# A token mixer's weight blocks on ScalarE's DMA queue, its products in another order, and later stages' loads further ahead

## The chip, the cores and the metric

The kernel runs on one core of one Trainium2 chip. A core has TensorE (matrix products), VectorE, ScalarE and GpSimd, and SyncE, which here only issues DMAs; ScalarE and GpSimd can issue DMAs too. Each engine works through its own instructions in a fixed order, and a wait of one instruction holds all behind it. The metric is the time of one execution on the device in microseconds.

## The reference

One encoder block on 1024 tokens of 1024 channels in float32: half a gated feed-forward layer, a mixer, another half of a feed-forward layer, a gated embedding, a norm. Cut to the mixer, which is what changes:

```python
u = rms_norm(h, mix_norm[i])
z = u @ w_in[i]                       # q | k | v | s_in | gates: 512 each, gates 2 x 1024
y_attn = neighbourhood_attention(q, k, v, na_rpb[i]) @ w_attn_out[i]   # 8 heads, 16 x 64 grid
y_ssm = s5_branch(s_in, ...) @ w_ssm_out[i]                            # scans in both directions
g_attn, g_ssm = jnp.split(jax.nn.sigmoid(gates), 2, axis=-1)
h = h + (g_attn * y_attn + g_ssm * y_ssm) @ w_out[i]

def s5_branch(s_in, ...):             # 32 groups of 16 channels, each a 64-dim complex state
    y = d_skip * u + forward scan + backward scan
    y = jax.nn.gelu(y)
    return y * jax.nn.sigmoid(y @ glu_w + glu_b)       # the gated unit
```

## The kernel before

Activations stand with channels on the 128 partitions and 512 tokens (one of two halves, t) on the free axis. Every float32 operand is split into a high and a low part (`split`: a cast on ScalarE, a subtraction on VectorE), and a product is three matmuls (`mm3`, lines 190 to 192): high x high, high x low, low x high.

The large products are done by a seven-product scheme on 2 x 2 blocks. In the mixer a "pair" is two column groups of `w_in` (q with k, or two gate groups), 12 pairs in all, and an item is one of the seven products of a pair: 84 items of 4 steps, a step being one `mm3`. Product i takes an activation operand `A7[i]`, a weight operand made by `b_operand` from four weight blocks (b11, b12, b21, b22; tile `blk`, 256 KB each), and adds into one of three PSUM banks:

```python
A7 = ("a12", "a11", "s1", "s2", "s4", "s3", "a22")
ACC7 = "ZXYXYXX"
NEW7 = (True, True, True, False, False, False, False)
```

Product 0 needs b21, product 1 b11, product 2 b12 - b11, 3 then b22 - b11, 4 b22, 5 b22 - b12, 6 b21 less what b11 became (`b_operand` changes the blocks in place, line 428 and 430). `s_evac` copies a finished bank or adds it to what was copied and hands results to `s_out`; q and k go to DRAM (`q_d`, `k_d`) from ScalarE's queue, the gates (`g_d`) from SyncE's. The stores wait in a list, `later`, which `s_store` issues in the third step of the next item. `s_ahead(n)` issues the block loads of items up to n + 4 (`s_load`, line 1490, SyncE's queue) and prepares weights up to n + 2 (`s_prep`). Blocks, prepared weights, results and much of attention's data share one pool of 24 buffers of 128 x 512 (tag "m"); a load waits until the buffer that it is given is free.

Between the steps of the items, side work runs from a generator, `mixer_side`: each step calls `tick`, and `yield n` lets n steps pass before the generator goes on. Its stages, in order:

- *injection*: for each of 16 pairs of state space groups, `inject_load` brings two tiles `fmi` and one `ut`, `inject` does eight small matmuls (`inj`); the scan then runs on GpSimd
- *attention*: 64 units (head, row block, column block). `attn_scores` does two matmuls `s`, VectorE adds the bias table `tb`, ScalarE does the exponential and the scaling (`sm`, lines 1236 and 1238); `attn_turn`, two units later, transposes (`pt`); `attn_values`, two more later, multiplies with v (`O`) and at a row block's end stores `ot` to `o_d` from ScalarE's queue
- *state space output*: per pair `ssm_load` (two tiles `emi`, one `ut`), `ssm_out` (copies `xs`, then six small matmuls a group pair, `yo`, and stores `ys` to `y_d`)
- *gated unit*: `glu_load` brings back `yt`, `glu_act` applies Gelu, `glu_half` multiplies with the weights `wgl` (loaded as `wgs`, 4 blocks for each half) into the banks `glu`, and stores `sg` to `y2_d`

`ready` tells attention which heads' q and k are stored, `drain` runs what is left of the generator at once. Tiles `ut`, `fmi`, `emi`, `tb`, `sm` and the transposes' copies share 12 buffers of 128 x 384 (tag "a"); `wgl` shares 2 with the keys (tag "k4"). Before the items, `values` computes v for both halves and stores it from ScalarE's queue; after them, `branches` (tile `br`) multiplies `o_d` and `y2_d`, brought by `load_br`, with the branches' weights.

TensorE's order is that of the program text. The order on the other engines, DMA issues included, is made by the tile framework's planner from priorities and a modelled time.

Of the kernel before, what the change touches and what calls it, by code (L numbers as in the profile page):

```python
# [9 lines left out]
F32R = mybir.dt.float32r  # L10
# [31 lines left out]
def encoder_block(ctx, tc, I, out):  # L42
# [151 lines left out]
    def hsl(t):  # L194
        return slice(t * HT, (t + 1) * HT)
# [997 lines left out]
    vdr = v_d.rearrange("h (r c) d -> h r c d", r=4)  # L1193
    vds = v_d.rearrange("h p (g a d) -> p g a h d", g=4, a=2)
    khl, qs, vld, tabs = {}, {}, {}, {}
    halves2 = slice(0, 64), slice(64, P)

    def load_k(hd):
# [52 lines left out]
    def attn_values(hd, rb, cb, O, ph, pl):  # L1251
        kp = 4 * KNC[cb]
        hl = vld[hd, cb]
        for g in range(3):

            T.matmul(O[:, ksl(cb)], lhsT=hl[0:kp, rb + g], rhs=ph[0:kp, ksl(g)], start=(g == 0), stop=False,
                     skip_group_check=True)
            T.matmul(O[0:64, ksl(cb)], lhsT=hl[0:kp, rb + g, 0:64], rhs=pl[0:kp, ksl(g)], start=False, stop=(g == 2),
                     skip_group_check=True)
        if cb == 3:  # L1260
            ot, ol = tmp("ot"), tmp("ol")
            A.copy(ol[0:64], O[64:128])
            V.tensor_tensor(ot[0:64].rearrange("p (r b c) -> p b r c", r=8, b=4),
                            O[0:64].rearrange("p (b r c) -> p b r c", b=4, r=8),
                            ol[0:64].rearrange("p (b r c) -> p b r c", b=4, r=8), ALU.add)
            nc.scalar.dma_start(o_d[hd * 64:(hd + 1) * 64, hsl(rb)], ot[0:64])


    ygs = {}
# [7 lines left out]
        for m in range(4):  # L1277
            A.activation(ygs[t, m], ygs[t, m], AF.Gelu_apprx_tanh)

    def glu_w(k):  # L1280
        w = ap_.tile([P, 2, HT], F32R, tag="k4", bufs=2, name="wgl")
        raw = tmp("wgs")
        nc.sync.dma_start(raw, I["wglu"][k])
        split(w[:, 0], w[:, 1], raw)
        return w

    def glu_half(t):
        os_ = [bank("glu") for _ in range(4)]
        for k in range(4):
            w = glu_w(k)  # L1290
            y = tmp("yh", dt=F32R), tmp("yl", dt=F32R)
            split(*y, ygs[t, k])
            yield 2
            for m in range(4):
                mm3(os_[m], (w[:, 0, ksl(m)], w[:, 1, ksl(m)]), y, k == 0, k == 3)
        for m in range(4):
            sg = tmp("sg")
            A.activation(sg, os_[m], AF.Sigmoid, bias=glub[:, m:m + 1])
            V.tensor_tensor(sg, sg, ygs.pop((t, m)), ALU.mult)
            nc.scalar.dma_start(y2_d[ksl(m), hsl(t)], sg)  # L1300
        yield 2
# [4 lines left out]
    def mixer_side():  # L1306
        yield from u_second()
        while 3 not in stored:
            yield 1
        yield 8  # L1310
        new_x()
        ld = {}
        for pr in range(2):
            ld[pr] = inject_load(pr)
        yield 6
        for pr in range(NPAIR):
            if pr + 2 < NPAIR:
                ld[pr + 2] = inject_load(pr + 2)
            inject(pr, *ld.pop(pr))
            yield 2  # L1320
        while 0 not in ready:
            scan_steps(1)
            yield 1
        units = [(hd, rb, cb) for hd in range(NH) for rb in range(2) for cb in range(4)]
        n = len(units)
        load_tab(0, 0)
        load_k(0)
        load_q(0, 0)
        for cb in range(4):
            load_v(0, cb)  # L1330
        for _ in range(6):
            scan_steps(1)
            yield 2
        sms, pts, O = {}, {}, {}
        lo, so = {}, {}
        for j in range(n + 5):
            if j < n:
                hd, rb, cb = units[j]
                b = 2 * hd + rb
                load_tab(b + cb // 2, (1, 2, 0, 0)[cb]) if cb < 3 else None  # L1340
                if cb == 1 and rb == 0:
                    load_q(hd, 1)
                if cb == 1 and rb == 1 and hd + 1 < NH:
                    while hd + 1 not in ready:
                        yield 1
                    load_q(hd + 1, 0)
                if rb == 0 and cb == 2 and hd + 1 in ready:
                    load_k(hd + 1)
                if rb == 1 and cb == 2 and hd + 1 < NH and hd + 1 not in khl:
                    load_k(hd + 1)  # L1350
                sms[j] = attn_scores(hd, rb, cb)
            if 0 <= j - 2 < n:
                pts[j - 2] = attn_turn(units[j - 2][2], sms.pop(j - 2))
            if 0 <= j - 4 < n:
                hd, rb, cb = units[j - 4]
                if cb == 0:
                    O[hd, rb] = bank("O")
                attn_values(hd, rb, cb, O[hd, rb], *pts.pop(j - 4))
                if rb == 1 and hd + 1 < NH:
                    load_v(hd + 1, cb)  # L1360
            scan_steps(2)
            if j >= n:
                lo[j - n] = ssm_load(j - n) if j - n < 3 else None
            yield 3
        scan_steps(NCH)
        for p in range(NPAIR + 1):
            if 3 <= p + 2 < NPAIR:
                lo[p + 2] = ssm_load(p + 2)
            if p < NPAIR:
                so[p] = ssm_out(p, *lo.pop(p))  # L1370
            if p > 0:
                so.pop(p - 1)()
            yield 1 + p % 2
        yield 3
        glu_load(0)
        yield 5
        glu_act(0)
        glu_load(1)
        yield 2
        glu_act(1)  # L1380
        for t in range(2):
            yield from glu_half(t)

    start(mixer_side())

# [30 lines left out]
    def values(t):  # L1416
        os_ = [bank("v") for _ in range(4)]
        for k in range(NK):
            load_wv()
            if t == 1 and k == 2:  # L1420
                s_ahead(-2)
            if t == 1 and k == 5:
                s_ahead(0)
            wh, wl = Wv[k]
            xs = U[("a11", "a12", "a21", "a22")[2 * t + k // 4]][k % 4]
            for i in range(4):
                xh, xl = (x[:, ksl(i)] for x in xs)
                T.matmul(os_[i], lhsT=xh, rhs=wh, start=(k == 0), stop=False)
                T.matmul(os_[i], lhsT=xh, rhs=wl, start=False, stop=False)
                T.matmul(os_[i], lhsT=xl, rhs=wh, start=False, stop=(k == NK - 1))  # L1430
                tick()
        for i in range(4):
            vh, vl = tmp("vh", dt=F32R), tmp("vl", dt=F32R)
            with tc.high_priority(offset=PRI):
                A.copy(vh, os_[i])
                V.tensor_tensor(vl, os_[i], vh.bitcast(F32), ALU.subtract)
            for j, x in enumerate((vh, vl)):
                nc.scalar.dma_start(vds[ksl(i % 2), 2 * t + i // 2, j], x.rearrange("p (h d) -> p h d", h=NH).bitcast(F32))
# [35 lines left out]


    pairs = [("qk", 0), ("qk", 1), ("g", 0), ("qk", 2), ("g", 1), ("qk", 3)] + [("g", m) for m in range(2, 8)]
    items = [(n, i) for n in range(len(pairs)) for i in range(7)]
    for n in range(7, len(items), 7):
        items[n - 1:n + 1] = items[n], items[n - 1]
    later = []  # L1480
    sblk, smade, sacc, sz = {}, {}, {}, {}

    def s_load(n, i):
        if i < 4:
            b = (2, 0, 1, 3)[i]
            kind, m = pairs[n]
            w = ((m, 4 + m) if kind == "qk" else (16 + 2 * m, 17 + 2 * m))[b % 2]
            blk = sblk.setdefault(n, [None] * 4)
            blk[b] = tmp("blk")
            nc.sync.dma_start(blk[b], win[w][:, hsl(b // 2)])  # L1490

    def s_prep(n, i):
        smade[n, i] = b_operand(sblk[n], i)
# [23 lines left out]
    def s_evac(n, i):  # L1517
        o = sacc
        z = sz.setdefault(n, {})
        if i in (0, 2, 3):  # L1520
            c, a = (("11", "Z"), None, ("22", "Y"), ("12", "X"))[i]
            z[c] = tmp("z" + c)
            A.copy(z[c], o[a])
            return
        c, a = {1: ("11", "X"), 4: ("12", "Y"), 5: ("22", "X"), 6: ("21", "X")}[i]
        if c != "21":
            V.tensor_tensor(z[c], o[a], z[c], ALU.add)  # L1527
        s_out(n, c, int(c[0]) - 1, int(c[1]) - 1, o[a] if c == "21" else z.pop(c))
# [6 lines left out]
    def s_run(n, i):  # L1535
# [4 lines left out]
        for k in range(4):  # L1540
            mm3(sacc[a], (hi[:, ksl(k)], lo[:, ksl(k)]), U[A7[i]][k], NEW7[i] and k == 0, k == 3, not NEW7[i])
            if k == 2:
                s_store()
                if i == 1 and n > 0 and pairs[n - 1][0] == "qk":
                    m = pairs[n - 1][1]
                    ready.update((2 * m, 2 * m + 1))
            tick()
# [23 lines left out]
    for n, item in enumerate(items):  # L1571
# [2 lines left out]
            for k in range(2):  # L1574
                u_put("s3", s3s.pop(0))
        if n == len(items) - 6:
            drain()
            oy[0].append(load_br(0, 0))
        if n == len(items) - 5:
            W0.append(load_was(0))  # L1580
            W0.append(load_was(1))
        if n == len(items) - 4:
            oy[0].append(load_br(0, 1))
        if n == len(items) - 3:
            oy[1].append(load_br(1, 0))
        if n == len(items) - 2:
            oy[1].append(load_br(1, 1))
        s_run(*item)
# [350 lines left out]
```

## Time and profile before

| what | us |
|---|---|
| median of 2 runs | 2140.22 (2139.58 to 2140.85) |
| profiled execution | 2141.12 |
| its span, first to last instruction | 2139.2 |
| TensorE busy in it | 2067.0 |
| VectorE, ScalarE, GpSimd busy | 1460.1, 1011.7, 436.4 |

PE is TensorE's matmuls, PEld its weight loads, DVE VectorE, ACT ScalarE, POOL GpSimd, SP SyncE; a q behind a name means that the engine's sequencer waits or issues a DMA. In rows of waits stands who waited for whom, the total in us, the number of times and the longest. In the chain of waits stand start, length and what. In rows of a tile stand minimum, median and maximum in ns, then the first and last start in us. In rows of a stretch stand its bounds, its length, busy us of PE, PEld, DVE, ACT and POOL with instructions, TensorE's granted clock, the DMA engines' busy share and GB/s. The mixer's items run from about 791 to 1213 us; injection goes before and into the values, attention runs from about 831 to 1081, the state space output to 1132, the gated unit to 1188.

### The profile page before, as it was taken

To read this page: it belongs to the slowest core of one execution; us is meant where nothing else is said; L and a number is where in the kernel's file an instruction comes from. 1 tells how busy PE (TensorE), PEld (TensorE's weight loads), DVE (VectorE), ACT (ScalarE), POOL (GpSimd) and SP (SyncE) were. 2 spreads that over 40 slices of the span, in tenths; PEclk is the share of its full clock that TensorE was granted. 3 is DMA by queue.
4 is the path that set the end of the run, shared out by engine and by line. 5 is a ranking of instruction groups with operands and counts; after the bars stand their busy time and mean duration, and the time that the engine had idled before them with its cause. 6 is when DMAs were issued, how large, how long until landed. Compare 5 with 4: busy or idle time off the path is not lost.

```text
span 2139.2 us, 28212 instructions
## 1 busy us (share of the span) xinstructions
PE 2067.0 (97%) x9518; PEld 1687.7 (79%) x9518; DVE 1460.1 (68%) x2470; ACT 1011.7 (47%) x1870; POOL 436.4 (20%) x656
## 2 busy tenths in 40 slices
PE   8999999999999988989987999999999999999998
PEld 3788888888888876778875788788888888888887
DVE  7897775766957736666643658896656565785855
ACT  6434333344445425667644646553333334545544
POOL 0037464640000528886000002000000000000000
PEclk9999999999999998999999999999999999999999
DMA  3435344484533576566667847142322328543302
GB/s 130 140 121 160 113 136 137 131 297 150 172 114 120 145 190 201 168 207 206 187 207 247 239 159 192 59 137 100 126 91 98 124 88 285 160 122 94 114 30 79
DMA packets 225521, 319.74 MB, mean 149 GB/s; under 512 B 53472, under 2 KB 93024, under 8 KB 225376
## 3 DMA queue, kind: packets, MB, share of 16 engines
q1 hardware_dynamic: 187664, 281.21, 41.9%
q10 hardware_dynamic: 35088, 31.49, 4.5%
q0 software_dynamic: 2624, 5.24, 1.3%
q8 instruction: 75, 1.23, 0.2%
q14 instruction: 70, 0.57, 0.1%
HBM read 224.01 MB, written 93.85 MB: 149 GB/s over the span
## 4 chain that ended last, share of the span: by engine, by line
PE 51%; DMA 7%; DVE 3%; ACT 2%; issue 1%; SPq 1%; ACTq 1%; DVEq 0%
DMA blk<-in_win 3%; PE dx L190 2%; PE dx L191 2%; PE dx L192 2%; PE ux L192 2%; PE gx L192 2%; PE gx L190 2%; PE ux L190 2%; PE ux L191 2%; PE gx L191 2%; PE br L190 1%; PE br L192 1%; PE br L191 1%; PE dy L191 1%; PE dy L192 1%; PE dy L190 1%
## 5 line engine op out<-in xcount | busy, mean ns | idle before, releaser
L159 ACT CAST wh<-hbuf 128x512 fp32r<-128x512 f32 x280 | 173.0, 622 | 390.7 <-PE gx L191 83.2
L160 DVE TENSOR_TENSOR wl<-hbuf,wh 128x512 fp32r<-128x512 f32 x280 | 209.9, 752 | 126.2 <-ACT wh L159 124.0
L159 ACT CAST wh<-wblk 128x512 fp32r<-128x512 f32 x190 | 118.1, 623 | 192.7 <-PE dx L191 82.3
L160 DVE TENSOR_TENSOR wl<-wblk,wh 128x512 fp32r<-128x512 f32 x190 | 130.9, 692 | 50.2 <-ACT wh L159 42.5
L190 PE MATMUL dx<-ah,wh 128*128 128x512 f32 x416 | 163.5, 393 | 0.4 <-DVE hbuf L694 0.3
L192 PE MATMUL dx<-ah,wl 128*128 128x512 f32 x416 | 161.9, 389 | 0.0
L191 PE MATMUL dx<-al,wh 128*128 128x512 f32 x416 | 161.8, 389 | 0.0
L160 DVE TENSOR_TENSOR al<-araw,ah 128x512 fp32r<-128x512 f32 x154 | 106.3, 694 | 50.1 <-PE dx L191 21.1
L190 PE MATMUL gx<-xh,wh 128*128 128x512 f32 x320 | 124.9, 390 | 1.2 <-DVE c L581 1.2
L190 PE MATMUL ux<-xh,wh 128*128 128x512 f32 x320 | 125.0, 391 | 0.0
L192 PE MATMUL ux<-xh,wl 128*128 128x512 f32 x320 | 124.5, 389 | 0.0
L192 PE MATMUL gx<-xh,wl 128*128 128x512 f32 x320 | 124.5, 389 | 0.0
L191 PE MATMUL gx<-xl,wh 128*128 128x512 f32 x320 | 124.5, 389 | 0.0
L191 PE MATMUL ux<-xl,wh 128*128 128x512 f32 x320 | 124.5, 389 | 0.0
L160 DVE TENSOR_TENSOR wl<-blk,wh 128x512 fp32r<-128x512 f32 x84 | 62.0, 739 | 80.8 <-ACT wh L159 76.6
L159 ACT CAST ah<-araw 128x512 fp32r<-128x512 f32 x154 | 95.0, 620 | 45.6 <-PE dx L191 14.2
L190 PEld LDWEIGHTS dx<-ah,wh 128*128 128x128 f32 x416 | 78.1, 188 | 18.6 <-DVE hbuf L694 1.2
L428 DVE TENSOR_TENSOR hbuf<-hbuf 128x512 f32<-128x512 f32 x120 | 91.1, 760 | 2.1
L191 PEld LDWEIGHTS dx<-al,wh 128*128 128x128 f32 x416 | 78.1, 188 | 16.6 <-issue 0.7
L192 PEld LDWEIGHTS dx<-ah,wl 128*128 128x128 f32 x416 | 78.1, 188 | 16.3
L1156 POOL TENSOR_TENSOR sc<-X,rho 128x128 f32<-128x128 f32 x128 | 76.4, 597 | 62.7 <-ACT X L1139 52.8
L190 PE MATMUL px<-xh,wh 128*128 128x512 f32 x192 | 80.4, 419 | 3.6 <-DVE z L1527 3.6
(397 smaller groups left out, 5729.0 us busy)
## 6 DMA issues: line engine op xcount, KB each, us to landing
araw<-a_d SPq DMA_DIRECT2D x154, 256.0 KB
a_d<-c SPq DMA_DIRECT2D x148, 256.0 KB
wblk<-in_wd SPq DMA_DIRECT2D x88, 256.0 KB
hbuf<-in_wg SPq DMA_DIRECT2D x40, 512.0 KB
hbuf<-in_wu SPq DMA_DIRECT2D x40, 512.0 KB
blk<-in_win SPq DMA_DIRECT2D x48, 256.0 KB
hbuf<-in_xT SPq DMA_DIRECT2D x32, 256.0 KB
h_d<-hbuf ACTq DMA_DIRECT2D x32, 256.0 KB
```

Source lines behind the costliest of these rows:

```text
L159: A.copy(hi, src)
L160: return eng.tensor_tensor(lo, src, hi.bitcast(F32), ALU.subtract)
L190: T.matmul(o, lhsT=wh, rhs=xh, start=first, stop=False, skip_group_check=more)
L191: T.matmul(o, lhsT=wh, rhs=xl, start=False, stop=False, skip_group_check=more)
L192: T.matmul(o, lhsT=wl, rhs=xh, start=False, stop=last, skip_group_check=more)
L428: V.tensor_tensor(b11, (b12, b22, None, None, b21)[i - 2], b11, ALU.subtract)
L1156: G.tensor_tensor(sc, both, rho4, ALU.mult)
```

## The change

Seven edits, all in the mixer: the weight blocks of the pairs are loaded from ScalarE's queue; the seven products of each pair run in the order 1, 2, 3, 4, 5, 0, 6 with `s_evac` made to fit, where they ran 0 to 6 with the last of a pair exchanged with the first of the next; attention's store of `ot` is issued one unit later, behind the next transposes (`late`); injection and state space output load three pairs ahead in place of two; the gated unit's weights are loaded by `glu_raw`, two ahead of their use, and its activation comes six steps later; the first block loads come two rounds earlier in the loop of `values` over k; at the end `drain` and the branch loads change places.

```diff
             V.tensor_tensor(ot[0:64].rearrange("p (r b c) -> p b r c", r=8, b=4),
...
-            nc.scalar.dma_start(o_d[hd * 64:(hd + 1) * 64, hsl(rb)], ot[0:64])
+            late.append((o_d[hd * 64:(hd + 1) * 64, hsl(rb)], ot[0:64]))
...
-    def glu_w(k):
-        w = ap_.tile([P, 2, HT], F32R, tag="k4", bufs=2, name="wgl")
+    def glu_raw(k):
         raw = tmp("wgs")
         nc.sync.dma_start(raw, I["wglu"][k])
+        return raw
+
+    def glu_w(raw):
+        w = ap_.tile([P, 2, HT], F32R, tag="k4", bufs=2, name="wgl")
         split(w[:, 0], w[:, 1], raw)
         return w
...
-    def glu_half(t):
+    def glu_half(t, raws):
         os_ = [bank("glu") for _ in range(4)]
         for k in range(4):
-            w = glu_w(k)
+            w = glu_w(raws.pop(0))
             y = tmp("yh", dt=F32R), tmp("yl", dt=F32R)
             split(*y, ygs[t, k])
+            if 4 * t + k < 6:
+                raws.append(glu_raw((k + 2) % 4))
             yield 2
@@ mixer_side @@
-        yield 8
+        yield 7
         new_x()
         ld = {}
-        for pr in range(2):
+        for pr in range(3):
             ld[pr] = inject_load(pr)
-        yield 6
+        yield 10
         for pr in range(NPAIR):
-            if pr + 2 < NPAIR:
-                ld[pr + 2] = inject_load(pr + 2)
+            if pr + 3 < NPAIR:
+                ld[pr + 3] = inject_load(pr + 3)
             inject(pr, *ld.pop(pr))
             yield 2
...
                 pts[j - 2] = attn_turn(units[j - 2][2], sms.pop(j - 2))
+            while late:
+                nc.scalar.dma_start(*late.pop())
...
         for p in range(NPAIR + 1):
-            if 3 <= p + 2 < NPAIR:
-                lo[p + 2] = ssm_load(p + 2)
+            if 3 <= p + 3 < NPAIR:
+                lo[p + 3] = ssm_load(p + 3)
...
         yield 3
         glu_load(0)
-        yield 5
+        raws = [glu_raw(0), glu_raw(1)]
+        yield 11
         glu_act(0)
         glu_load(1)
         yield 2
         glu_act(1)
         for t in range(2):
-            yield from glu_half(t)
+            yield from glu_half(t, raws)
@@ values @@
-            if t == 1 and k == 2:
+            if t == 1 and k == 0:
                 s_ahead(-2)
...
-    items = [(n, i) for n in range(len(pairs)) for i in range(7)]
-    for n in range(7, len(items), 7):
-        items[n - 1:n + 1] = items[n], items[n - 1]
+    items = [(n, i) for n in range(len(pairs)) for i in (1, 2, 3, 4, 5, 0, 6)]
@@ s_load @@
-            nc.sync.dma_start(blk[b], win[w][:, hsl(b // 2)])
+            nc.scalar.dma_start(blk[b], win[w][:, hsl(b // 2)])
@@ s_evac @@
-        if i in (0, 2, 3):
-            c, a = (("11", "Z"), None, ("22", "Y"), ("12", "X"))[i]
+        if i in (1, 2, 3):
+            c, a = (("11", "X"), ("22", "Y"), ("12", "X"))[i - 1]
             z[c] = tmp("z" + c)
             A.copy(z[c], o[a])
             return
-        c, a = {1: ("11", "X"), 4: ("12", "Y"), 5: ("22", "X"), 6: ("21", "X")}[i]
+        c, a = {0: ("11", "Z"), 4: ("12", "Y"), 5: ("22", "X"), 6: ("21", "X")}[i]
@@ s_run @@
-                if i == 1 and n > 0 and pairs[n - 1][0] == "qk":
+                if i == 2 and n > 0 and pairs[n - 1][0] == "qk":
@@ the loop over the items @@
         if n == len(items) - 6:
-            drain()
             oy[0].append(load_br(0, 0))
...
         if n == len(items) - 4:
+            oy[1].append(load_br(1, 0))
+        if n == len(items) - 3:
+            drain()
             oy[0].append(load_br(0, 1))
-        if n == len(items) - 3:
-            oy[1].append(load_br(1, 0))
```

More of the change, by code (lines that the diff above doesn't have):

```diff
@@ L1195, in encoder_block @@
     khl, qs, vld, tabs = {}, {}, {}, {}
+    late = []
     halves2 = slice(0, 64), slice(64, P)
@@ L1334, in mixer_side @@
         sms, pts, O = {}, {}, {}
+        late.clear()
         lo, so = {}, {}
@@ L1362, in mixer_side @@
             if j >= n:
-                lo[j - n] = ssm_load(j - n) if j - n < 3 else None
+                if j - n < 3:
+                    lo[j - n] = ssm_load(j - n)
             yield 3
```

## The prediction

> **What bounds the kernel now.** I read the busy shares first, then what TensorE waits for, then the stretches, then the chain of waits.
>
> ```profile
> PE 2067.0 (97%) x9518; PEld 1687.7 (79%) x9518; DVE 1460.1 (68%) x2470; ACT 1011.7 (47%) x1870; POOL 436.4 (20%) x656
> ```
>
> TensorE is busy nearly all the time, so only time in which it stands or runs slowly can be won. The waits of the whole kernel, by the matmul that waited and what released it (total us, times, longest):
>
> ```profile
> PE pt L1245 <- ACT sm L1238: 12.8, 8, 4.5
> PE glu L190 <- ACT wgl L159: 12.1, 3, 11.1
> PE yo L1182 <- DMA ut<-u_d: 6.3, 5, 2.1
> PE pz L190 <- ACT wh L159: 5.1, 1, 5.1
> ...
> PE inj L1132 <- DMA ut<-u_d: 3.0, 4, 1.1
> PE py L190 <- ACT wh L159: 3.0, 1, 3.0
> PE py L190 <- ACT z L1523: 1.6, 1, 1.6
> ...
> PE yo L1182 <- DMA emi<-e_d: 1.2, 1, 1.2
> ```
>
> All of these tiles belong to the mixer, the part that is changed; with the 3.6 us of `px`, which stand in the next fence, they add up to 48.7 us. A wait costs more than itself, as the matmul groups and the stretches show (the last columns are granted clock, DMA share, GB/s):
>
> ```profile
> L191 PE MATMUL dx<-al,wh 128*128 128x512 f32 x416 | 161.8, 389 | 0.0
> L190 PE MATMUL px<-xh,wh 128*128 128x512 f32 x192 | 80.4, 419 | 3.6 <-DVE z L1527 3.6
> ```
> ```profile
> 791.00:831.00 40.00, 35.34 (x147) 27.92 (x146) 24.32 (x34) 16.51 (x29) 34.91 (x66) 0.96 0.74 214
> 831.00:1081.00 250.00, 230.07 (x1329) 196.50 (x1328) 157.58 (x388) 160.45 (x366) 146.64 (x303) 0.95 0.65 195
> 1081.00:1132.00 51.00, 41.23 (x268) 35.24 (x267) 17.83 (x46) 22.92 (x55) 0.00 (x0) 1.00 0.70 210
> 1132.00:1151.00 19.00, 7.89 (x36) 6.22 (x34) 6.70 (x11) 10.79 (x17) 0.00 (x0) 0.84 0.97 333
> 1151.00:1189.00 38.00, 36.95 (x149) 29.10 (x150) 17.55 (x28) 16.28 (x27) 0.00 (x0) 0.94 0.47 156
> 1189.00:1213.00 24.00, 20.36 (x84) 16.36 (x83) 19.17 (x28) 15.82 (x26) 0.00 (x0) 0.94 1.01 266
> ```
>
> The same matmul takes 389 ns in the feed-forward parts and 419 on average here: behind a gap the clock is lowered. The lost clock is 1.6 + 12.5 + 0 + 3.0 + 2.3 + 1.4 = 20.8 us (stretch times one minus clock). Some of it lies inside the gaps and is free, so its cost is between 0 and 20.8; I take 13 (7.5 of it in attention's stretch, 2 behind the gated unit's gap, the rest elsewhere). The ceiling for this change is thus about 48.7 + 13 = 62 us, 2.9% of the time.
>
> The chain of waits says what stands behind "ACT sm" and "ACT wh" (start, us, what):
>
> ```profile
> 827.54 11.82 DMA blk<-in_win
> ...
> 876.10 10.05 DMA blk<-in_win
> ...
> 1076.52 3.95 DMA blk<-in_win
> ```
>
> A weight block takes 10 to 12 us in attention's stretch, although one needs 3.95 us at 1076. ScalarE or VectorE waits for the block in its own order, and the softmax steps for the next transpose (`sm`, then `pt`) stand behind it.
>
> **The change part by part.** *Blocks on ScalarE's queue.* SyncE loses 48 issues, ScalarE gains 48.
>
> ```profile
> L1490 SPq DMA_DIRECT2D blk<-in_win x48: 323/380/2063, 771.1 to 1174.7; - x48
> ```
> ```profile
> L1533 ACTq DMA_DIRECT2D k_d<-qkh x8: 326/327/484, 811.7 to 983.3; - x8
> L1438 ACTq DMA_DIRECT2D v_d<-vl x8: 366/1162/2049, 757.3 to 797.5; - x8
> ```
>
> An issue of full rows on ScalarE takes 327 ns, so 48 are 15.7 us. ScalarE is busy 160.45 of 250 us there, so they find room; I cost them at 0, and at 15.7 if none is hidden. The transfer leaves the queue where keys, queries, values, tables and gate stores stand ahead of it, and shares its new queue with the stores of q, k, v and the attention output. Its new time is not in the trace: between the 3.95 us of the block that met little traffic and the 11.82 us of the slowest. I take 6, nearer to the first, because the DMA engines are busy 0.65 of that stretch and not full. Attention's gaps that lead back to a block (pt 12.8, pz 5.1) are 4.5 us or less apiece, bar one of 5.1; 4 us less for a block closes most of them. I count 12 of the 17.9 us, leaving 6 for VectorE, for ScalarE's own order and for blocks that were late by their buffer and not by their transfer, and with it 4 us of clock: **16 us**; bounds 0 (a loss is the third rival) and 25.4, which is 17.9 and all 7.5.
>
> The Trainium skill, page "DMA: Bandwidth & Descriptors", section "Rules for kernel authors", speaks against this: transfers issued from several engines run on the same 16 DMA engines, and spreading them does not add bandwidth. By it this term would be 0; it is the second rival below. The same page's section "Queues, rings and completion order" says that each DMA engine takes turns between the queues that have work, which would favour the 6 us; no run here shows which holds.
>
> *ScalarE as the waiting engine.* A block's issue waits until its buffer is free. These waits stood on SyncE (first and last of 24 rows of the stretch from 729 to 1215, 37 us in sum):
>
> ```profile
> SPq L1490 <- DMA vhl<-v_d: 8.3, 3, 5.6
> ...
> SPq L1490 <- ACT wh L159: 0.2, 1, 0.2
> ```
>
> On ScalarE whatever is queued behind such a wait stands too: weight casts, exponentials, transposes' copies, on all of which TensorE waits. I count it inside the 6 us left above; the bound is the third rival.
>
> *Product order.* Every pair now runs 1, 2, 3, 4, 5, 0, 6. Counts of casts, copies and additions stay: product 1 is copied where product 0 was, product 0 is added where 1 was. The block b21 (number 2) is loaded and needed four steps later. The last k result is stored one product (12 matmuls) earlier against the key load that waits for it, a wait of SyncE alone. I take 0, bounds -3 (the block of product 0 of the first pair, now behind the value stores at 1.16 us an issue) and +3. The first two `py` waits (3.0 and 1.6) come behind those value issues on ScalarE; nothing takes them away: 0.
>
> *Late attention store.* It moves the issue behind the next unit's softmax and transpose. 16 issues; 0, bounds 0 and 3.
>
> *Injection.* Three pairs ahead in place of two: three buffers a pair, four pairs in flight, 12 buffers, which is what the pool has. The waits are 1.1 us at most, less than the two product steps and eight small matmuls that pass between two pairs: **2.5 us** of 3.0; bounds 0 and 3.
>
> *State space output.* Three pairs ahead again, but here the pair before is still unfinished when the next load is issued, five pairs or 15 buffers for 12. The load of pair q therefore still waits until pair q - 4 is done, as before; SyncE already waited there. I count **4 us** of 7.5, from the blocks that leave its queue; bounds 0 and 7.5.
>
> ```profile
> SPq L1165 <- PE yo L1182: 3.9, 2, 3.1
> ```
>
> *Gated unit.* The chain ahead of its first matmul, one of its steps of a matmul at full clock, and the times of its inputs (first to last start):
>
> ```profile
> 1144.16 6.09 DMA wgs<-in_wglu
> ...
> 1209.22 0.23 PE px L191
> ```
> ```profile
> L1186 ACT COPY ys<-yo x16: 368/373/374, 1083.7 to 1131.0; 128x256 f32<-128x256 f32 x16
> L160 DVE TENSOR_TENSOR yl<-yt,yh x8: 683/686/693, 1144.0 to 1179.6; 128x512 fp32r<-128x512 f32 x8
> ```
>
> The weights were loaded only at 1144.16. Loaded two ahead, they are no longer last; next are the activations, split at 1144.0 + 0.7 = 1144.7, 13.7 us behind the last state space copy (1131.0). TensorE's work between: 13 steps before (1 + 3 + 5 + 2 + 2), 19 now, at 3 x 0.23 us a step: 9.0 and 13.1 us. So 0.6 us of the 11.1 stay; I count 8 of the 12.1 and 2 of clock, since the weights of later steps still wait for two shared buffers: **10 us**; bounds 0 and 15.
>
> *The tail.* The six steps come off the cover behind the unit.
>
> ```profile
> L192 PE MATMUL glu<-yh,wgl x32: 389/389/628, 1152.0 to 1187.7; 128*128 128x512 f32 x32
> L160 DVE TENSOR_TENSOR bl<-br,bh x16: 655/870/1233, 1188.7 to 1218.5; 128x512 fp32r<-128x512 f32 x16
> ```
>
> From its last matmul to the last split of its output are 1218.5 + 0.9 - 1188 = 31 us. Behind it stood 84 matmuls (the row of 1189 to 1213 above), 28 steps; six fewer are 22, at 0.69 us 15.2. With the 16 steps of attention's branch (11.0) and 8 of the first half's second branch (5.5) they make 31.7, so it is just covered; each us less would cost one. The `px` wait of 3.6 stays. 0, bounds -5 and +5.
>
> Sum: 16 + 2.5 + 4 + 10 = 32.5 us. The profiled execution took 2141.1 (span 2139.2 and 1.9 around it), the median of the runs is 2140.2, so they stand for each other: 2140.2 - 32.5 = 2107.7; I say **2107**.
>
> **Rivals.** *Everything is covered.* A block in its own queue takes about 4 us, and no gap outlives it: 3.0 + 17.9 + 7.5 + 12.1 = 40.5, and 11 of clock with ScalarE's order no hindrance, in all some 52 to 55: **2087**. For it: the block of 3.95 us. Against: the 37 us of buffer waits do not vanish, they move.
>
> *The blocks do not come sooner.* If they are limited by the shared engines or by their buffers, attention gains nothing: 2.5 + 4 + 10 = 16.5 and **2124**. For it: DMA share 0.65 to 0.74 and 37 us of buffer waits. Against: the loads that now stand ahead of a block in SyncE's one queue, and the 3.95 us of the block that had few.
>
> *ScalarE is blocked: slower.* Each wait at a block's issue holds the exponentials behind it. If three quarters of the 37 us reach TensorE (28) with a quarter more for the clock (13 to 48.7 is about that), 35 us are lost, 16.5 won: **2159**. It decides from 13 us of such waits on (16.5 / 1.25). For it: ScalarE's order is fixed, and the value stores ahead of the first products already hold it for 1.2 us each. Against: it idles a third of the stretch.
>
> **How the numbers follow.** Main 0.42 (2094 to 2118), covered 0.25, not sooner 0.20, blocked 0.13. Two per cent is 42.8 us (about what a measurement of this kernel can tell from no change), so the bounds are 2097.4 and 2183.0. Faster: nearly all of "covered" and a quarter of the main case, 0.33. Slower: the far end of "blocked", 0.02. Within: 0.65. The range runs from 2083, under "covered", to 2140; outside are the best of "covered" (0.07) and most of "blocked".
>
> **What would show it.** Right: block waits of ScalarE and VectorE gone, `pt` waits under 7 us, the clock of attention's stretch at 0.97 or more, the 11.1 us gap under 2, `inj` near 0, `yo` still several us. Wrong: ScalarE standing at the block's issue line, `pt` or `py` waits grown, or a new gap at the branch products. What makes the number wrong most likely is the time of a block in its new queue, which nothing here shows.

## Result and the profile after

The changed kernel took 2118.78 us (median of 2 runs, 2116.88 to 2120.67), the kernel before 2140.22: ratio 0.990, interval 0.9857 to 0.9942, 21 us or 1.0% less. Forecast were 2107 and a range of 2083 to 2140. Run again beside other kernels (below) the ratio was 0.9912 (0.9893 to 0.9932), which is 19 us. The kernel before was run again with each group of experiments, and its median moved between 2136 and 2140 us from group to group, so the experiments are read by their ratios to it. The traces of the two kernels differ by more than the medians do, 24.1 us in their spans: the profiled execution of the kernel before was among its slower ones, that of the changed kernel among its faster ones. What follows from this pair of traces is therefore some 3 to 5 us more than the change is worth.

TensorE's waits, the same view as before (line numbers from 1209 on are 1 to 9 higher):

```profile
PE pt L1246 <- ACT sm L1239: 15.0, 7, 7.5
...
PE yo L1182 <- DMA ut<-u_d: 3.6, 6, 1.0
PE px L190 <- ACT z L1532: 3.4, 2, 3.2
PE glu L190 <- ACT yh L159: 3.0, 2, 2.4
PE inj L1132 <- DMA ut<-u_d: 2.5, 2, 2.0
PE glu L191 <- DVE yl L160: 2.0, 3, 0.9
PE yo L1182 <- DMA emi<-e_d: 1.6, 1, 1.6
...
PE glu L190 <- ACT wgl L159: 1.2, 1, 1.2
PE yo L1184 <- ACT ys L1186: 1.2, 1, 1.2
...
PE px L190 <- DVE z L1536: 0.8, 1, 0.8
```

The 11.1 us in front of the gated unit are 2.4, and the 3.6 us at the tail are 0.8. `inj` stands nearly as it was (2.5 for 3.0); the waits of `yo` for loads are 5.2 for 7.5. The transposes' waits, the largest row, have not fallen in sum (12.8 before). The row of `pz` is gone, but its wait is not: it stood at 840 us, and at about the same place in the order of work, at 846, the changed kernel has the 7.5 us of `pt`. Together `pz` and `pt` went from 17.9 to 15.0. The stretches show what was won all the same:

```profile
831.00:1081.00 250.00, 233.18 (x1393) 200.71 (x1393) 161.83 (x403) 163.91 (x378) 147.26 (x299) 0.97 0.68 205
1075.00:1130.00 55.00, 47.67 (x282) 39.70 (x280) 20.13 (x46) 28.74 (x65) 0.00 (x0) 1.00 0.80 246
1130.00:1170.00 40.00, 33.60 (x139) 25.76 (x140) 19.71 (x32) 19.23 (x33) 0.00 (x0) 1.00 0.59 207
1170.00:1196.00 26.00, 24.91 (x110) 20.03 (x108) 13.97 (x23) 12.32 (x22) 0.00 (x0) 1.00 0.97 271
```

In the same 250 us TensorE now does 1393 matmuls where it did 1329, at a clock of 0.97 for 0.95; behind attention the clock stays at 1.00, where three stretches had 0.84, 0.94 and 0.94. One can also follow the start of each item through both traces. The changed kernel is level up to attention's start (item 12), 11.2 us ahead at item 60 (near attention's end), 13.6 at item 72, 22.9 at item 78 (the gated unit), 24.4 at the first branch product and 24.1 at the end of the span.

How much of this is waiting and how much is clock can be read between the same items. From item 12 to item 60 the time went from 237.0 to 226.0 us: gaps between matmuls of over 0.2 us went from 19.8 to 15.3, and the time lost to a lowered clock (length times one minus clock) from 13.7 to 6.8. So of attention's 11 us less than half are waits, and the larger part is clock. From item 60 to item 78 it went from 122.6 to 111.0 us, gaps from 21.9 to 13.6 and lost clock from 5.1 to 0; there the two overlap.

The blocks, and what stands in the chain of waits:

```profile
L1499 ACTq DMA_DIRECT2D blk<-in_win x48: 329/340/2088, 765.2 to 1168.7; - x48
```
```profile
827.43 14.39 DMA vhl<-v_d
842.33 0.63 ACT wh L159
...
949.67 4.44 DMA blk<-in_win
...
1029.92 7.38 DMA blk<-in_win
...
1044.53 6.46 DMA blk<-in_win
```

No block takes 10 us any more; the longest of all 48 is 7.4. The longest wait left (7.5 us from 838 on) leads back to a value load.

### The profile page after: what moved, and what is told of

It is laid out like the page before. It is cut to its first block, busy times and chain, and to the rows that moved or that the text cites. A ratio compares the mean times of both kernels' runs of the same rounds, so it can differ in the third digit from the quotient of the medians.

```text
span 2115.1 us, 28193 instructions
## 1 busy us (share of the span) xinstructions
PE 2059.3 (97%) x9518; PEld 1680.8 (79%) x9518; DVE 1458.8 (69%) x2470; ACT 1010.1 (48%) x1870; POOL 437.9 (21%) x656
## 4 chain that ended last, share of the span: by engine, by line
PE 82%; DMA 7%; DVE 6%; ACT 2%; issue 1%; SPq 1%; ACTq 0%; DVEq 0%
PE dx L190 4%; PE dx L191 4%; PE dx L192 4%; PE gx L190 3%; PE ux L190 3%; PE gx L191 3%; PE ux L192 3%; PE ux L191 3%; PE gx L192 3%; PE dy L192 2%; PE dy L190 2%; PE dy L191 2%; PE gy L190 2%; PE uy L190 2%; PE uy L192 2%; PE gy L192 2%
## 5 line engine op out<-in xcount | busy, mean ns | idle before, releaser
L159 ACT CAST ah<-araw 128x512 fp32r<-128x512 f32 x154 | 95.0, 619 | 43.8 <-PE dx L191 14.2
L192 PEld LDWEIGHTS dx<-ah,wl 128*128 128x128 f32 x416 | 78.1, 188 | 16.3
```

The costliest lines, as they stand in the source:

```text
L159: A.copy(hi, src)
L192: T.matmul(o, lhsT=wl, rhs=xh, start=False, stop=last, skip_group_check=more)
```

## Experiments

### The queue: taken back, and alone

```diff
 # e1: the changed kernel with
-            nc.scalar.dma_start(blk[b], win[w][:, hsl(b // 2)])
+            nc.sync.dma_start(blk[b], win[w][:, hsl(b // 2)])
 # e2: the kernel before with the opposite edit and nothing else
```

> The changed kernel with the weight blocks' loads back on SyncE's queue, all else kept. In the two traces attention's stretch is 11 us shorter after the change. Theory (the queue is what shortened it): about 2130 us, 10 to 12 us over the changed kernel, with block waits of ScalarE and VectorE back at 10 to 12 us a block. Rival (the product order, which spreads the loads, did it): about 2119 us, as the changed kernel.

> The kernel before with the blocks' loads on ScalarE's queue alone. Theory: attention's gain comes alone, about 2129 us (2140 - 11). Rival (ScalarE held at the block's issue line costs what the shorter transfer wins, and only the new order makes room): 2140 us or more.

Measured: queue back 0.9957 (0.9943 to 0.9971), queue alone 0.9958 (0.9942 to 0.9975). So the queue alone is worth 0.42%, 9 us, and taking it back costs about as much (from 0.9912 to 0.9957, 10 us). The stretch of attention, first with the queue back, then with the queue alone:

```profile
831.00:1081.00 250.00, 227.23 (x1326) 194.21 (x1325) 156.03 (x390) 156.67 (x362) 150.92 (x307) 0.96 0.65 195
```
```profile
831.00:1081.00 250.00, 235.82 (x1404) 202.63 (x1403) 163.23 (x403) 165.66 (x379) 145.63 (x299) 0.98 0.68 205
```

1326 matmuls against 1404. By the start of item 60 the kernel with the queue alone is 11.6 us ahead of the one before, and the changed kernel with the queue taken back 2.8 behind it. So the whole gain of attention comes and goes with this one edit. Both theories hold; the rivals (the product order did it, or ScalarE is held for as long as the transfer wins) fall.

A semaphore is a counter on which engines wait. Each block's DMA shows 16 counts on its semaphore as it lands; from the issue of each block to its sixteenth count, for the blocks issued between 831 and 1075 us, the traces give:

| kernel | blocks | mean us | longest us |
|---|---|---|---|
| before | 29 | 5.9 | 11.4 |
| queue back | 30 | 6.4 | 12.5 |
| queue alone | 30 | 5.0 | 7.9 |
| changed | 31 | 5.1 | 7.4 |

With the queue alone the mean falls by under 1 us, the longest by 3.5; in the other pair, queue back against changed, by over 1 and by 5. Of the 29 blocks before, 5 took over 8 us, and 8 of the 30 with the queue back; with the blocks on ScalarE's queue none did. VectorE and ScalarE together waited 39.1 us for blocks before and 55.4 with the queue back, but 23.9 with the queue alone and 23.1 in the changed kernel (29.3 in its second trace). So the few late blocks are what went.

One rival was not tried by itself: the edit also takes 48 issues and their waits away from SyncE, so that its other loads can be issued sooner. Little speaks for it. In the kernel before TensorE waited only 1.8 us for keys, queries and values, which SyncE still loads, and in attention's stretch VectorE waited 13.3 us for the bias tables before and 10.2 with the queue alone.

### The gated unit's loads alone

```diff
 # e3: the kernel before with
+        raws = [glu_raw(0), glu_raw(1)]
-        yield 5
+        yield 11
...
-            w = glu_w(k)
+            w = glu_w(raws.pop(0))
...
+            if 4 * t + k < 6:
+                raws.append(glu_raw((k + 2) % 4))
```

> The kernel before with the gated unit's weights loaded two ahead and its activation six steps later, nothing else. Theory: the 11.1 us wait and its slow clock go, the tail stays covered: about 2130 us (9 to 11 us less). Rival (the wait is only taken over by the activations, or comes back in the tail because six steps of cover are gone): 2136 to 2140 us.

Measured: 0.9966 (0.9952 to 0.998), 7.3 us less. In its trace:

```profile
PE pt L1245 <- ACT sm L1238: 13.6, 7, 4.4
PE pz L190 <- ACT wh L159: 5.3, 1, 5.3
...
PE px L190 <- ACT bh L159: 4.5, 1, 4.5
...
PE glu L190 <- ACT wgl L159: 1.5, 1, 1.5
...
PE glu L190 <- ACT yh L159: 1.3, 1, 1.3
PE glu L191 <- DVE yl L160: 1.2, 2, 0.9
```

The 12.1 us are 4.0 (1.5 + 1.3 + 1.2). The tail's wait is 4.5 in place of 3.6, so next to nothing comes back there. Attention is untouched (level at item 60 within 1 us). The theory holds, with 7 us for the 9 to 11 that it gave; the rival falls.

### The product order: alone, and taken back

```diff
 # e4: the kernel before with (and s_evac and the index in s_run to match); e5: the changed kernel without it
+    items = [(n, i) for n in range(len(pairs)) for i in (1, 2, 3, 4, 5, 0, 6)]
```

> The kernel before with the products in the order 1, 2, 3, 4, 5, 0, 6 and the evacuation made to fit, nothing else. Theory (order is worth nothing by itself): 2140 us within 3 us. Rival (it is the order that shortened attention, by an earlier store of k and evenly spread loads): about 2130 us.

> The changed kernel with the products in their old order, all else kept. The order alone made the kernel before 0.2% faster, chiefly at its end. Theory (the order gives its few us here too): about 4 to 6 us slower than the changed kernel, ratio to the kernel before near 0.993. Rival (together with the queue the order is worth nothing, or costs): ratio 0.990 or less.

Measured: alone 0.9978 (0.9961 to 0.9994), 4.7 us less; taken back 0.9921 (0.9905 to 0.9938), whose interval overlaps that of the changed kernel (0.9912), so there a loss of 2 us is seen and not shown. Of the expectations for e4 neither was right: the order is not worth nothing (its interval is 1 to 8 us, though the theory's 3 us lie inside), and it is not attention that gains. By item starts the kernel with the order alone is level with the one before at item 60 (0.6 us behind) and 8.3 us ahead at the first branch product, 5 of them from item 78 on; at the tail its trace has no wait of TensorE between 1189 and 1213 us, where before had 3.6. With the order taken back that wait is there again:

```profile
PE px L190 <- DVE z L1538: 3.7, 1, 3.7
```

The last pair's products now end with 0 and 6 and need other evacuations than before, behind the branch loads' splits; which of these frees VectorE was not tried.

### Loads three pairs ahead alone

```diff
 # e6: the kernel before with
-        yield 8
+        yield 7
...
-        for pr in range(2):
+        for pr in range(3):
...
-        yield 6
+        yield 10
...
-            if pr + 2 < NPAIR:
-                ld[pr + 2] = inject_load(pr + 2)
+            if pr + 3 < NPAIR:
+                ld[pr + 3] = inject_load(pr + 3)
...
-            if 3 <= p + 2 < NPAIR:
-                lo[p + 2] = ssm_load(p + 2)
+            if 3 <= p + 3 < NPAIR:
+                lo[p + 3] = ssm_load(p + 3)
```

> The kernel before with injection and state space output loading three pairs ahead in place of two, nothing else. Prediction's terms: 2.5 us at the injection and, without the queue's help, 0 to 4 us at the output: ratio 0.997 to 0.999. Rival (the twelve buffers bind, so loads go no earlier): 1.000, with the yo waits at 7 us and the inj waits at 2 to 3 us as before.

Measured: 0.9993 (0.9982 to 1.0003), no difference that shows.

```profile
PE yo L1184 <- ACT ys L1186: 4.4, 3, 3.1
...
PE yo L1184 <- ACT xs L1176: 3.8, 1, 3.8
...
PE inj L1132 <- DMA ut<-u_d: 1.9, 2, 1.4
```

`inj` loses 1.1 us. In the state space output the waits for loads are gone from the list, and waits for ScalarE's copies stand there in their place: 8.2 us (4.4 + 3.8) against the 7.5 for loads before. The late loads were covered, and the next engine was late.

### The three small edits alone

```diff
 # e11: the kernel before with the late store, s_ahead at k == 0, and at the end,
 # beside the branch loads' new places,
-            drain()
...
+        if n == len(items) - 3:
+            drain()
```

> The kernel before with only the three small edits: attention's store one unit later, the first block loads two rounds earlier in the values, drain and branch loads exchanged at the end. Prediction's terms: 0, with bounds of about 5 us either way: ratio 0.998 to 1.002. Rival (they carry a part of the gain that the queue, the gated unit's loads and the order do not explain): 0.997 or less.

Measured: 1.0011 (0.9998 to 1.0024): nothing, as predicted. The parts alone add up to 9.0 + 7.3 + 4.7 + 1.5 - 2.4 = 20 us, the whole is 19 to 21. So no dependence between the parts shows; one of a few us could hide, since each part is known only to some 3 us.

### What holds the rest: blocks on GpSimd's queue

```diff
 # e7: the changed kernel with
-            nc.scalar.dma_start(blk[b], win[w][:, hsl(b // 2)])
+            nc.gpsimd.dma_start(blk[b], win[w][:, hsl(b // 2)])
 # e8: nc.scalar for n < 7, nc.gpsimd from there on
```

The sequencer's idle time ahead of the 48 block issues, added up from the traces, was 37.0 us on SyncE before and 15.6 us on ScalarE after. That ScalarE is held there was the theory for the waits that are left.

> The changed kernel with the weight blocks' loads on GpSimd's queue, which has semaphores of its own and holds neither ScalarE nor SyncE. Theory (what is left of attention's waits comes in good part from ScalarE held at its DMA issues, 15.6 us at the blocks): attention's pt waits fall from 15 us to under 8, glu's from 6.2 to under 3, total 8 to 12 us under the changed kernel, ratio near 0.985. Rival (a block from GpSimd's queue is slow, 7 us and more to landing, and stands behind the scan's steps, so blocks come late): ratio 0.995 or more, with long waits for blocks.

> The changed kernel with the blocks of the last five pairs, loaded when the scan on GpSimd is over, on GpSimd's queue and the others on ScalarE's. Theory (ScalarE was held 6.1 us at 1137.7 at a block's issue, behind loads of SyncE's queue that count on the same semaphore): the glu waits fall from 6.2 us to under 3, attention stays, total about 4 us under the changed kernel, ratio near 0.988. Rival (the activations are late by themselves): glu waits and total as in the changed kernel.

Measured: e7 0.9911 (0.9892 to 0.9929), e8 0.9922 (0.9906 to 0.9937), both as the changed kernel (0.9912). The theory of e7 falls, and so does its rival, since the ratio is not 0.995 and TensorE has no long wait behind a block. With ScalarE free of blocks the trace of e7 shows:

```profile
PE pt L1246 <- ACT sm L1239: 9.8, 6, 2.8
PE yo L1182 <- DMA ut<-u_d: 5.1, 5, 1.9
...
PE yo L1182 <- issue: 3.2, 2, 1.9
...
PE s L1230 <- DMA qh<-q_d: 3.0, 1, 3.0
PE glu L191 <- DVE yl L160: 2.1, 2, 1.2
PE glu L190 <- ACT wgl L159: 2.0, 1, 2.0
...
PE s L1230 <- DMA ql<-q_d: 1.4, 2, 1.0
```

The 7.5 us wait of `pt` is gone, and TensorE waits 3.0 for query loads at about the same place instead; `pt` and `s` together are 14.2, where they were 15.0. A block took 5.9 us in the mean there and 8.1 at the longest: the mean is that of the kernel before, the longest is not, and the gain stayed. In e8 the one long hold at the gated unit went, as its theory said. Among ScalarE's waits from 1125 to 1152 us the changed kernel has this row and e8 has none like it:

```profile
ACT wh L159 <- DMA hbuf<-h_d: 6.5, 1, 6.5
```

The waits of `glu` in e8 came to about 4 us from 6.2, but the total did not move, as its rival said.

### Loads further ahead, and a burst spread out

```diff
 # e9: the changed kernel with
-    LL, LP = 4, 2
+    LL, LP = 5, 2
 # e10: the changed kernel with
-        for cb in range(4):
-            load_v(0, cb)
-        for _ in range(6):
+        for cb in range(6):
+            if cb < 4:
+                load_v(0, cb)
             scan_steps(1)
             yield 2
```

> The changed kernel once more, beside the next three on one chip, so that differences of a few us can be told. Both theories: ratio to the kernel before 0.988 to 0.992.

> The changed kernel with the weight blocks loaded five items ahead in place of four. Theory (what is left of attention's waits is blocks issued too late, since a block now lands in 5 us): pt waits fall from 15 us to under 10, 4 to 7 us less than the changed kernel. Rival (the waits come from VectorE's and ScalarE's own order and from buffers, which one more block in flight makes scarcer): no change or up to 5 us more.

> The changed kernel with attention's first four value loads spread over the six scan steps behind the first key and query loads, not issued at once. Theory (the 7.5 us wait at 838 comes from ScalarE's stores and blocks standing behind the first value load, which took 14.4 us to land in a burst of loads): that wait falls under 4 us, total 3 to 5 us less than the changed kernel. Rival (it only moves to another load of the burst): pt and s waits together stay at 15 us, total as the changed kernel.

Measured on one chip: changed kernel 0.9912 (0.9893 to 0.9932), five ahead 0.9912 (0.9894 to 0.9931), values spread 0.9909 (0.9891 to 0.9927). No difference. Five ahead, `pt` fell, within what was expected, and ScalarE's copies of results took the place:

```profile
PE pt L1246 <- ACT sm L1239: 9.7, 7, 4.1
PE px L190 <- ACT z L1532: 6.8, 2, 4.6
```

against, in the changed kernel run beside it,

```profile
PE pt L1246 <- ACT sm L1239: 11.6, 6, 7.0
...
PE px L190 <- ACT z L1532: 3.8, 2, 3.2
```

With the values spread the wait at attention's start was 6.4 us, where the theory had under 4, so the burst's shape is not its cause, or not alone. One lead was not followed: each of the 32 value loads shows its landing in 5 counts, where a block's DMA shows 16; whether this goes with their slow landing is open. What makes up the last 10 to 15 us of attention's waits is open: taking away ScalarE's hold, the late issue and the burst, one at a time, each only changed which row they stand in.

## Why the prediction was right, and where its terms were off

The direction, the place and two mechanisms were right: attention's gain is that of the queue, and the gated unit's that of its loads. The size was 19 to 21 us for 32.5, so the measured time lies nearer to the second rival's 2124 than to 2107. The number alone would not have told the two apart; the queue alone at 0.9958 does, since that rival gives attention nothing. It is also in part luck that the total came as near as it did: 4.7 us come from the product order, a term put at 0. Term by term (the parts alone, by their ratios times 2137 us):

| term | predicted | measured | interval |
|---|---|---|---|
| blocks on ScalarE's queue | 16 | 9.0 | 5 to 12 |
| gated unit | 10 | 7.3 | 4 to 10 |
| injection and state space output | 2.5 + 4 | 1.5 | -1 to 4 |
| product order | 0 | 4.7 | 1 to 8 |
| small edits | 0 | -2.4 | -5 to 0 |

*The blocks* were mis-sized, and the step is "4 us less for a block closes most of them", with 12 us of waits counted. The late blocks did lose their 4 us (11.4 to 7.4 at the longest), and "I take 6" was near (5.1 in the mean). But the waits of `pt` and `pz` together fell from 17.9 only to 11.8 with the queue alone, and to 15.0 and 11.6 in the two traces of the changed kernel: 3 to 6 us of the 12. In the changed kernel the three gaps of 2.2 to 2.3 us are replaced by four of 1.6 or less. The two largest did not close: the 4.5 us at 888 became 3.0, and at attention's start the wait is longer than before, because ScalarE there stood behind a value load next. The clock, put at 4 us, gave more than that (13.7 to 6.8 us lost, above). The sentence "a weight block takes 10 to 12 us in attention's stretch" read the chain of waits as if it showed the usual block; it shows the latest ones, since only these release anything on the chain. The mean was 5.9 us already.

*ScalarE held at the block's issue* was real, but smaller than the bound: of 37 us on SyncE 15.6 are left on ScalarE, and taking all of them away in e7 won nothing. The third rival's mechanism is there, and its cost does not show. The reading "a block's issue waits until its buffer is free" was wrong for a good part of the 37 us: rows of 14.4 us name the landing of a load (8.3 of them `vhl`), which frees no buffer. What such an issue waits for stands in the last section.

*The second rival* falls, as said. The Trainium skill's rule that transfers of several engines share the same 16 DMA engines (page "DMA: Bandwidth & Descriptors", section "Rules for kernel authors") is not against this: the bytes hardly flow faster (195 to 205 GB/s in attention's stretch). That the DMA engines take turns between queues (the Trainium skill, same page, section "Queues, rings and completion order") would fit the longest block falling from 11.4 to 7.9 us while the mean lost under 1: a block no longer stands behind all that SyncE issued ahead of it. No run here shows that this is the reason.

*The gated unit* kept 6.2 us of waits (3.0 + 2.0 + 1.2) where 4.1 were left for it (12.1 - 8). About 2 of them came from ScalarE, held for 6.1 us at a block's issue, since e8 took that hold away and kept 4.1; the ready time of 1144.7 did not reckon with it. The 10 us predicted lie at the edge of what was measured. *The state space output* had its limit named ("15 buffers for 12"), yet 4 us were counted; the waits for loads fell by 2.3 in the changed kernel, and where they went altogether, in e6, ScalarE's copies, which the step did not ask about, were late next. *The product order* at 0 missed the tail, which lies past the stage where its steps were followed; b21, moreover, is needed six products later (from the second pair on), not "four steps".

*The clock*: the waits fell by 58.2 - 41.9 = 16.3 us over the whole span (gaps between matmuls over 0.2 us, added up in both traces), the span by 24.1; the other 8 us are matmuls at a higher clock. The sum had counted 26.5 us of waits and 6 of clock. So what failed is the waits, and not the clock. The granted clock of the runs agrees: over the whole span its median was 0.989 in 17 runs of the kernel before and 0.993 in the 5 runs of the changed kernel beside them, and 0.004 of 2137 is 8.5 us.

Of the signs that the prediction named, the clock of attention's stretch (0.97) and `yo` (still several us) came as written, and no new gap stands at the branch products. The 11.1 us gap is 2.4, a little over the 2 named. The others failed: `pt` under 7 stayed at 15, `inj` near 0 at 2.5, and the block waits of ScalarE and VectorE, which were to be gone, went from 39.1 to 23.1 us.

## What to carry to other kernels

The chain of waits names the latest instances of a transfer, not its usual time: take the mean over all its issues, and count how many are late. A wait does not close just because what ended it comes sooner: ask what would end it next. Here the same place in the order of work was taken over by another engine or another load at attention's start, in the state space output and in two later trials, each time without the gain that was counted. A load can gain from another queue even when bandwidth does not rise; here it was worth 9 us at 195 to 205 GB/s. And where gaps go, look at the clock: it gave 8 of the 24 us between the two traces.

## What was not expected of the chip and the program

In this program the DMAs of SyncE's and ScalarE's queues count on the same eight semaphores, and in the traces an issue waits until the DMA ahead of it on its semaphore has landed, whichever queue that came from: of the 48 block issues 43 wait for the very semaphore that they count on, in the issue itself or in the waiting instructions right ahead of it (all 48 before). So the block issued on ScalarE at 841.9 stood until the value load of SyncE's queue, issued at 827.43, had landed 14.39 us later. Moving a load to another engine's queue did not free it from slow loads of the first. GpSimd's DMAs count on eight semaphores of their own.
